# The lower halves of the last FFN's down weights: VectorE subtraction or accumulating DMA

## The chip, the cores and the metric

The kernel runs on one core of a Trainium2 chip. The metric is device time in microseconds (us) for one execution, the median of several runs. The core has four engines that matter here, each with its own instruction stream: TensorE (PE in the profile, with its weight loads as PEld), VectorE (DVE), ScalarE (ACT) and GpSimd (POOL). SyncE (SP) only issues DMAs. Engines wait for one another and for DMAs through semaphores. Sixteen DMA engines serve all queues of the core.

## The reference

The model is a two-layer decoder trunk on 256 tokens with a width of 2048. Layer 0 mixes by causal pooling, layer 1 by latent attention; each layer ends in a SwiGLU feed-forward network (FFN) with 5632 hidden columns. All tensors are float32. What matters for this change is the FFN:

```python
def swiglu(h, w_gate, w_up, w_down):
    return (jax.nn.silu(h @ w_gate) * (h @ w_up)) @ w_down
...
for i in range(DEPTH):
    ...
    h = modulate(rmsnorm(x, norm_ffn[i]), shift_f, scale_f)
    x = x + gate_f[:, None, :] * swiglu(h, ffn_gate[i], ffn_up[i], ffn_down[i])
return rmsnorm(x, final_norm)
```

## The kernel before

**Products in halves.** A weight matrix is read in units of 512 by 512, laid out as 128 partitions of 2048 float32 values, which is 1 MiB. TensorE multiplies in the type float32r, which keeps fewer bits than float32, so each operand is split: the upper half `hi` is the value rounded to float32r, and the lower half `lo` is the value less `hi`. A product is the sum of three: activation's upper half times `hi`, its lower half times `hi`, its upper half times `lo`. A unit therefore costs 3 parts x 4 slices of 128 x 2 token tiles = 24 matmuls of 128x512 at L420, and in each unit the eight that read `lo` come last. Only in the last unit of a sum they come earlier: there the two token tiles are done one after the other.

**How a unit gets ready.** `w_unit` (L382) takes one of the six `raw` buffers, has SP load the unit into it (L387) and calls `split` (L370). That takes two of the six `hl` buffers, lets ACT write `hi` as a copy of `raw` (L374), and lets DVE write `lo = raw - hi` (L376). Six `hl` buffers hold three units: the one in use and two ahead. A `raw` buffer comes free when both halves are made.

**The FFN of a layer.** There are 11 hidden chunks of 512 columns. The steps stand in a list by hand: `FFN_STEPS`, in which p is the gate and up projection of a chunk, t its transposition on TensorE, and d the down projection of a group of chunks. `GROUPS` has chunks 0 to 2, 3 to 5, 6 to 8, and 9 to 10:

```python
FFN_STEPS = "p0 p1 t0 p2 t1 p3 t2 p4 p5 d0 t3 t4 p6 t5 d1 p7 t6 p8 t7 p9 t8 d2 p10 t9 d3".split()
GROUPS = ([0, 1, 2], [3, 4, 5], [6, 7, 8], [9, 10])
```

A step `down(i)` loops over four output columns of 512 and, within each, over the chunks of the group, and adds the products of one column in two banks of PSUM (one for each token tile). Groups 0, 1 and 2 have 12 units each. After a column the banks go to the sums in `x`: by ACT in group 0 (L762), by DVE in the others (L764).

**Background work.** `split` begins with `tick()`, which at a planned rate issues other work: `Part.unit` loads 1 MiB of `mod_wt` into a `raw` buffer on the same SP queue (L210) and has DVE multiply and sum it (L211). In the last FFN this goes on until step p8. Two loads of the residual stream that was set aside (L613) fall into the time of d2 and p10.

**Order.** A scheduler places the instructions on each engine by priority; the halves have a raised one, and every engine runs its stream in order. POOL has little to do in the whole program: 30 busy instructions. Its only DMAs spread three gate rows (L297).

Of the kernel before, what the change touches and what calls it, by code (L numbers as in the profile page):

```python
# [9 lines left out]
F32 = mybir.dt.float32  # L10
# [3 lines left out]
AF = mybir.ActivationFunctionType  # L14
ALU = mybir.AluOpType
# [11 lines left out]
DEPTH = 2  # L27
# [31 lines left out]
GROUPS = ([0, 1, 2], [3, 4, 5], [6, 7, 8], [9, 10])  # L59
# [34 lines left out]
def tile_trunk(ctx: ExitStack, tc: tile.TileContext, a: dict, out: bass.AP):  # L94
    nc = tc.nc
    sync, act, dve, pe, pool = nc.sync, nc.scalar, nc.vector, nc.tensor, nc.gpsimd
# [7 lines left out]
    def nm(s):  # L104
        n_names[0] += 1
        return f"{s}_{n_names[0]}"

    def raw_t(shape, dt=F32):
        return work.tile(shape, dt, tag="raw", bufs=6, name=nm("raw"))

    def hl_t(shape, dt=F32R):
        return work.tile(shape, dt, tag="hl", bufs=6, name=nm("hl"))

    def act_t(shape, dt=F32R):
        return work.tile(shape, dt, tag="act", bufs=8, name=nm("act"))
# [10 lines left out]
    def ps_t():  # L126
        return psum.tile([P, CH], F32, tag="ps", name=nm("ps"))
# [195 lines left out]
    def pump(n):  # L323
        with tc.issue_after(behind[-1]) if behind else nullcontext():
            for _ in range(min(n, len(background))):
                background.pop(0).unit()
# [15 lines left out]
    def tick():  # L342
        credit[0] += rate[0]
        while credit[0] >= 1.0 and not held[0]:
            credit[0] -= 1.0
            if len(background) > goal[0]:
                pump(1)
# [8 lines left out]
    def flush(*ins):  # L356
        if not ins:
            while pending:
                pending.pop(0)[1]()
            return  # L360
        todo = [f for wait, f in pending if wait == 0]
        pending[:] = [(wait - 1, f) for wait, f in pending if wait]
        with ExitStack() as queue:
            for i in ins:
                queue.enter_context(tc.issue_after(i.ins))
            for f in todo:
                f()


    def split(r, shape):  # L370
        tick()
        hi, lo = hl_t(shape), hl_t(shape)
        with tc.high_priority(offset=100):
            hi_ins = act.activation(hi, r, AF.Copy)  # L374
        with tc.high_priority(offset=100):
            lo_ins = dve.tensor_tensor(out=lo, in0=r, in1=hi.bitcast(F32), op=ALU.subtract)  # L376
        flush(hi_ins, lo_ins)
        return hi, lo

    early, w_load = {}, [None]  # L380

    def w_unit(src):  # L382
        if repr(src) in early:
            return early.pop(repr(src))
        shape = [P, KL, CH]
        r = raw_t(shape)
        w_load[0] = sync.dma_start(r.rearrange("p k n -> p (k n)"), src)  # L387
        return split(r, shape)

    class Halved:  # L390
# [303 lines left out]
    def ffn_weights(l):  # L694
        return a["ffn_gate"][l], a["ffn_up"][l], a["ffn_down"][l]
# [40 lines left out]
    def ffn(l, hT, gate_name, begun, then):  # L736
        wd = ffn_weights(l)[2]
        mids, nat = {}, {}

        def project(c, which):  # L740
            if c in begun:
                begun[c][which].block(ND - 1, hT[ND - 1])
                return begun[c][which].result()
            return proj(ffn_weights(l)[which][:, c], hT)

        def transposed(c):
            m = act_t([P, 2, KL, T])
            for tok in range(NT):
                pt = ps_t()
                for f in range(KL):  # L750
                    pe.transpose(pt[:, f * P:(f + 1) * P], nat[c][tok][:, f * P:(f + 1) * P], ident)  # L751
                v = pt.rearrange("p (f t) -> p f t", f=KL)
                ts_ = slice(tok * P, (tok + 1) * P)
                act.activation(m[:, 0, :, ts_], v, AF.Copy)  # L754
                dve.tensor_tensor(out=m[:, 1, :, ts_], in0=v, in1=m[:, 0, :, ts_].bitcast(F32), op=ALU.subtract)  # L755
            mids[c] = m

        stream_end = []

        def gather(bank, sums, first):  # L760
            if first:
                act.activation(sums, bank, AF.Copy)  # L762
            else:
                dve.tensor_tensor(out=sums, in0=bank, in1=sums, op=ALU.add)  # L764

        def down(i):
            g = GROUPS[i]
            last = g[-1] == NF - 1
            if last:
                stat_start()  # L770
                end = stream_end[0]
                end.start(gates[gate_name])
            for j in range(ND):
                js = slice(j * CH, (j + 1) * CH)
                banks = [ps_t() for _ in range(NT)]
                if last and j == 0:
                    hold()
                if last and j == ND - 1:
                    weights = [w_unit(wd[c, j]) for c in g]
                    if l < DEPTH - 1:  # L780
                        then([(mids[c], hi, lo, c == g[0]) for c, (hi, lo) in zip(g, weights)], banks,
                             lambda tok: end.piece(banks[tok], tok, j))
                        continue
                    for tok in range(NT):
                        ends = tok == NT - 1
                        if not ends:
                            for c, (hi, lo) in zip(g, weights):
                                proj_unit(banks, mids[c], hi, lo, c == g[0], c == g[-1], (tok,))
                            end.piece(banks[tok], tok, j)
                            end.finish(tok)  # L790
                            end.rest_of(tok + 1)
                            continue

                        order = [(mids[c], w, i, k) for c, (hi, lo) in zip(g, weights)
                                 for w, i in ((hi, 0), (hi, 1), (lo, 0)) for k in range(KL)]
                        for bank, hs in ((banks[tok], slice(0, CH // 2)), (ps_t(), slice(CH // 2, CH))):
                            for n, (m, w, i, k) in enumerate(order):
                                pe.matmul(bank[:, :hs.stop - hs.start], lhsT=m[:, i, k, tok * P:(tok + 1) * P],
                                          rhs=w[:, k, hs], start=n == 0, stop=n == len(order) - 1)
                            end.section(bank, tok, hs)  # L800
                        end.finish_fast(tok)
                    continue
                for c in g:
                    hi, lo = w_unit(wd[c, j])
                    turning = last and j == 0 and c == g[0]
                    proj_unit(banks, mids[c], hi, lo, c == g[0], c == g[-1],
                              between=(lambda: transposed(g[-1])) if turning else None)
                for tok in range(NT):
                    if last:
                        pending.append((0, lambda bank=banks[tok], tok=tok, j=j: end.piece(bank, tok, j)))  # L810
                    else:
                        pending.append((0, lambda bank=banks[tok], sums=x[:, tok, js]: gather(bank, sums, i == 0)))

        def project_chunk(c):
            if c == ASIDE:
                stream_aside(l)
            if c == NF - 1:
                end = StreamEnd(l)
                stream_end.append(end)
                for n, wait in enumerate(KNOWN):  # L820
                    pending.append((wait, lambda n=n: end.known(n // NT, n % NT, gates[gate_name])))
            gb = project(c, GATE)
            nat[c] = []
            for tok in range(NT):
                sg = t2k([P, CH])
                pending.append((0, lambda sg=sg, bank=gb[tok]: act.activation(sg, bank, AF.Silu)))  # L826
                nat[c].append(sg)
            ub = project(c, UP)
            for tok in range(NT):
                dve.tensor_tensor(out=nat[c][tok], in0=ub[tok], in1=nat[c][tok], op=ALU.mult)  # L830

        for step in FFN_STEPS:
            {"p": project_chunk, "t": transposed, "d": down}[step[0]](int(step[1:]))
# [100 lines left out]
    scale = Strips(1, False, lambda v: with_bias(cols[:, C_AM0, :], v, 1, vcol[:, V_NM:V_NM + KD]))  # L934
# [451 lines left out]
    for j in range(ND):  # L1386
        if len(hmx) < ND:
            hidden_q()
        hi, lo = w_unit(a["w_dq"][j, 0])
# [132 lines left out]
    for g in range(3):  # L1522
        if g > 0:
            project_heads(g - 1)
        r, q_h, q_l = head_weights(g)
        uq[g] = q_h, q_l
        tick()
        with tc.high_priority(offset=100):
            hi_ins = act.activation(q_h, r, AF.Copy)
# [201 lines left out]
```

## Time and profile before

| What | Value |
|---|---|
| Median of 3 runs | 1903.12 us (1901.91 to 1905.33) |
| Profiled execution: span, first to last instruction | 1901.2 us |
| PE busy | 1850.5 us (97%) |
| DVE busy | 1418.4 us (75%) |
| ACT busy | 834.6 us (44%) |
| POOL busy | 21.7 us (1%) |
| DMA, over the span | 575.49 MB, mean 303 GB/s |

The profiled execution has no time of its own beside its span, the time from its first to its last instruction; that span lies 1.9 us under the median of the runs.

Reading it: each row of a group of instructions names the line, the engine and the operation, then the tiles written and read, the shape, the count, the busy time, the mean time of one in nanoseconds, and the idle time of the engine before them with what ended it. PE's busy time comes from modelled ends, since matmuls overlap; so a row can show 390 ns for a matmul while a new one starts sooner. A table by stretches of time gives, for each stretch, the busy us of each engine (with the number of instructions), the granted TensorE clock, the mean busy share of the 16 DMA engines, and the GB/s that they moved. "SPq" and "POOLq" are the queues on which DMAs are issued.

### The profile page before, as it was taken

What the parts mean: (1) busy time and instruction counts of PE and PEld (TensorE: products, weight loads), DVE (VectorE), ACT (ScalarE), POOL (GpSimd) and SP (SyncE); (2) the same over time, 40 slices, a digit from 0 to 9 for tenths busy, and PEclk for the clock granted to TensorE, in tenths of its full rate; (3) what the DMA queues carried; (4) which work ended last, traced back from release to release, by engine and by line L of the source; (5) the groups of instructions that cost most, each with busy time, mean ns of one, the idle gap of its engine ahead of it and who ended that gap; (6) DMA issues with size and microseconds to landing.
All of it is one profiled execution on the core that took longest, in us unless ns stands there. A gap on an engine that the chain in (4) does not pass through costs nothing.

```text
span 1901.2 us, 21797 instructions
## 1 busy us (share of the span) xinstructions
PE 1850.5 (97%) x8733; PEld 1501.9 (79%) x8733; DVE 1418.4 (75%) x1411; ACT 834.6 (44%) x914; POOL 21.7 (1%) x30
## 2 busy tenths in 40 slices
PE   7689999999999999999999999999999999999998
PEld 2256888888888888888889888888888888888886
DVE  1247799999889788897898886889785565644556
ACT  3125643453433343345776645634444433333343
POOL 0000000000000000000110000000000000000000
PEclk9989999999999999999999999999999999999999
DMA  9999998889999899994694585988776666655551
GB/s 399 417 419 410 381 368 332 317 308 375 411 351 394 341 381 360 392 418 178 221 368 164 185 324 223 385 321 335 260 268 243 245 242 243 246 219 201 220 199 44
DMA packets 80118, 575.49 MB, mean 303 GB/s; under 512 B 8929, under 2 KB 9361, under 8 KB 11281
## 3 DMA queue, kind: packets, MB, share of 16 engines
q1 hardware_dynamic: 79346, 570.68, 77.7%
q0 software_dynamic: 432, 3.15, 0.4%
q8 instruction: 68, 1.11, 0.2%
q10 hardware_dynamic: 240, 0.29, 0.0%
q14 instruction: 32, 0.26, 0.0%
HBM read 567.76 MB, written 6.32 MB: 302 GB/s over the span
## 4 chain that ended last, share of the span: by engine, by line
PE 94%; DMA 5%; ACT 0%; DVE 0%; SPq 0%; issue 0%; POOLq 0%; DVEq 0%; ACTq 0%
PE ps L420 80%; DMA raw<-in_mod_w_dram 4%; PE ps L429 2%; PE ps L1001 2%; PE ps L256 2%; PE ps L1354 1%; PE ps L751 1%; PE ps L1440 1%; PE ps L1546 1%; PE ps L1257 1%; DMA raw<-in_mod_block_dram 0%; PE ps L562 0%; PE ps L1443 0%; PE ps L196 0%; PE ps L1455 0%; PE ps L1495 0%
## 5 line engine op out<-in xcount | busy, mean ns | idle before, releaser
L420 PE MATMUL ps<-hl,act 128*128 128x512 f32 x6672 | 1522.6, 390 | 0.7 <-ACT act L754 0.7
L420 PEld LDWEIGHTS ps<-hl,act 128*128 128x128 f32 x6672 | 1250.8, 188 | 259.5 <-ACT act L754 0.9
L374 ACT ACTIVATE hl<-raw 128x2048 fp32r<-128x2048 f32 x285 | 545.5, 1918 | 644.7 <-PE ps L420 444.8
L376 DVE TENSOR_TENSOR hl<-raw,hl 128x2048 fp32r<-128x2048 f32 x285 | 652.2, 2290 | 234.0 <-ACT hl L374 232.2
L211 DVE SCALAR_TENSOR_TENSOR raw<-raw,s_row 128x2048 f32<-128x2048 f32 x168 | 383.4, 2285 | 1.3 <-DMA raw<-in_mod_wt_dram 1.2
L256 PE MATMUL ps<-raw,s_strip 128*32 128x512 f32 x392 | 59.0, 692 | 36.4 <-DMA raw<-in_mod_w_dram 35.4
L720 DVE TENSOR_TENSOR act<-ps,act 128x512 f32<-128x512 f32 x96 | 64.5, 685 | 17.9 <-PE ps L420 17.8
L256 PEld LDWEIGHTS ps<-raw,s_strip 128*32 128x32 f32 x392 | 9.1, 116 | 66.3 <-DMA raw<-in_mod_w_dram 43.3
L429 PE MATMUL ps<-hl,act 128*128 128x512 f32 x192 | 47.6, 400 | 0.6 <-DVE act L525 0.5
L429 PEld LDWEIGHTS ps<-hl,act 128*128 128x128 f32 x192 | 35.1, 188 | 10.3 <-ACT act L512 2.5
L754 ACT ACTIVATE act<-ps 128x512 fp32r<-128x512 f32 x44 | 23.7, 591 | 41.1 <-PE ps L751 29.0
L764 DVE TENSOR_TENSOR x<-ps,x 128x512 f32<-128x512 f32 x32 | 21.7, 690 | 23.1 <-PE ps L420 23.1
L542 DVE TENSOR_TENSOR hl<-raw,hl 128x2048 fp32r<-128x2048 f32 (+3 forms) x17 | 31.9, 1879 | 4.8 <-ACT hl L539 4.7
L830 DVE TENSOR_TENSOR t2k<-ps,t2k 128x512 f32<-128x512 f32 x24 | 16.5, 689 | 24.5 <-PE ps L420 24.5
L263 DVE COPY t2k<-ps 128x256 f32<-128x256 f32 x4 | 1.7, 425 | 44.0 <-ACT t2k L262 44.0
L826 ACT ACTIVATE t2k<-ps 128x512 f32<-128x512 f32 x24 | 14.2, 591 | 46.4 <-PE ps L420 46.4
L1001 PEld LDWEIGHTS ps<-act,act 128*128 128x128 f32 x128 | 24.4, 197 | 11.5 <-issue 8.4
L449 ACT ACTIVATE junk<-x 128x512 bf16<-128x512 f32 x23 | 14.4, 627 | 41.0 <-DVE x L634 23.9
L718 ACT ACTIVATE act<-ps 128x512 f32<-128x512 f32 x32 | 19.1, 596 | 29.2 <-PE ps L420 29.2
L1001 PE MATMUL ps<-act,act 128*128 128x256 f32 x128 | 31.5, 398 | 0.0
L755 DVE TENSOR_TENSOR act<-ps,act 128x512 fp32r<-128x512 f32 x44 | 28.4, 684 | 2.5 <-ACT act L754 2.5
L539 ACT ACTIVATE hl<-raw 128x2048 fp32r<-128x2048 f32 (+1 forms) x15 | 26.5, 1766 | 3.5 <-PE ps L420 3.5
(230 smaller groups left out, 984.7 us busy)
## 6 DMA issues: line engine op xcount, KB each, us to landing
raw<-in_mod_wt_dram SPq DMA_DIRECT2D x136, 1024.0 KB, 6.1
raw<-in_ffn_up_dram SPq DMA_DIRECT2D x88, 1024.0 KB, 5.5
raw<-in_ffn_down_dram SPq DMA_DIRECT2D x88, 1024.0 KB, 5.4
raw<-in_ffn_gate_dram SPq DMA_DIRECT2D x87, 1024.0 KB, 5.5
raw<-in_mod_w_dram SPq DMA_DIRECT2D x48, 1024.0 KB, 13.5
raw<-in_kv_mod_wt_dram SPq DMA_DIRECT2D x32, 1024.0 KB, 7.8
raw<-in_w_o_dram SPq DMA_DIRECT2D x16, 1024.0 KB, 5.4
raw<-in_mod_block_dram SPq DMA_DIRECT2D x8, 1024.0 KB, 12.5
```

Source lines behind the costliest of these rows:

```text
L211: dve.scalar_tensor_tensor(out=r, in0=r, scalar=1.0, in1=s_row, op0=ALU.mult, op1=ALU.mult, accum_out=self.sums[:, self.n:self.n + 1])
L256: pe.matmul(self.bank[m * STRIP:(m + 1) * STRIP, :], lhsT=weights(k), rhs=r[:, k, i, :], start=first, stop=last)
L374: hi_ins = act.activation(hi, r, AF.Copy)
L376: lo_ins = dve.tensor_tensor(out=lo, in0=r, in1=hi.bitcast(F32), op=ALU.subtract)
L420: pe.matmul(banks[tok], lhsT=t_[:, i, k, tok * P:(tok + 1) * P], rhs=w[:, k, :], start=first and n < len(part), stop=last and n >= len(ord ...
L429: pe.matmul(bank, lhsT=t_[:, i, k, tok * P:(tok + 1) * P], rhs=w[:, k, :], start=first and n == 0, stop=last and n == len(order) - 1)
L539: hid_ins[0] = act.activation(w[1], w[0], AF.Copy)
L542: dve.tensor_tensor(out=w[2][:, ks], in0=w[0][:, ks], in1=w[1][:, ks].bitcast(F32), op=ALU.subtract)
L720: dve.tensor_tensor(out=part, in0=banks[tok], in1=part, op=ALU.add)
L754: act.activation(m[:, 0, :, ts_], v, AF.Copy)
L755: dve.tensor_tensor(out=m[:, 1, :, ts_], in0=v, in1=m[:, 0, :, ts_].bitcast(F32), op=ALU.subtract)
L1001: pe.matmul(mixed[g][:, n % 2, :], lhsT=wp[g][:, k, ns], rhs=pool_all[g // 2][:, g % 2, k, :], start=k == 0, stop=k == KL - 1)
```

## The change

For the last layer's groups 0, 1 and 2, which is 36 units, a flag sends `w_unit` another way. SP loads the unit into `raw` as before and ACT writes `hi` as before. Then ACT writes `lo` too, as the negated `hi` (a copy from SBUF to SBUF with scale -1), and POOL issues a DMA that reads the same 1 MiB of weights from HBM again and adds it to `lo` in place. DVE's subtraction of these units is gone. Group 3, the projections and the first FFN keep the old way.

```diff
+    by_dma = [False]
...
         w_load[0] = sync.dma_start(r.rearrange("p k n -> p (k n)"), src)
+        if by_dma[0]:
+            tick()
+            hi, lo = hl_t(shape), hl_t(shape)
+            with tc.high_priority(offset=100):
+                hi_ins = act.activation(hi, r, AF.Copy)
+                act.activation(lo, hi.bitcast(F32), AF.Copy, scale=-1.0)
+                pool.dma_start(lo.rearrange("p k n -> p (k n)"), src, accum_op=ALU.add)
+            flush(hi_ins)
+            return hi, lo
         return split(r, shape)
...
         def down(i):
+            by_dma[0] = l == DEPTH - 1 and i < len(GROUPS) - 1
...
+            by_dma[0] = False
```

The streams of PE and SP keep their instructions and their order. On ACT, five units of d1 stand like this before:

```order
L374 ACTIVATE hl_11002<-raw_11000 128x2048
L374 ACTIVATE hl_11034<-raw_11032 128x2048
L374 ACTIVATE hl_11067<-raw_11062 128x2048
L374 ACTIVATE hl_11099<-raw_11097 128x2048
L374 ACTIVATE hl_11131<-raw_11129 128x2048
```

And the same five units of d1 on ACT now (L393 writes `hi`, L394 the negated copy):

```order
L393 ACTIVATE hl_11017<-raw_11015 128x2048
L394 ACTIVATE hl_11018<-hl_11017 128x2048
L393 ACTIVATE hl_11050<-raw_11048 128x2048
L394 ACTIVATE hl_11051<-hl_11050 128x2048
L393 ACTIVATE hl_11084<-raw_11079 128x2048
L394 ACTIVATE hl_11085<-hl_11084 128x2048
L393 ACTIVATE hl_11117<-raw_11115 128x2048
L394 ACTIVATE hl_11118<-hl_11117 128x2048
L393 ACTIVATE hl_11150<-raw_11148 128x2048
L394 ACTIVATE hl_11151<-hl_11150 128x2048
```

Each unit has two ACT instructions in place of one, the second right behind the first. On DVE, at the same place of d1, the subtractions stand among evictions (L764) and background work (L211) before:

```order
L376 TENSOR_TENSOR hl_11035<-raw_11032,hl_11034 128x2048
L764 TENSOR_TENSOR x<-ps_10903,x 128x512
L764 TENSOR_TENSOR x<-ps_10904,x 128x512
L376 TENSOR_TENSOR hl_11068<-raw_11062,hl_11067 128x2048
L211 SCALAR_TENSOR_TENSOR raw_11193,sums_9830<-raw_11193,s_row 128x2048
L376 TENSOR_TENSOR hl_11100<-raw_11097,hl_11099 128x2048
L376 TENSOR_TENSOR hl_11132<-raw_11129,hl_11131 128x2048
```

On DVE in d1 now, only the evictions and the background work are left:

```order
L774 TENSOR_TENSOR x<-ps_10915,x 128x512
L211 SCALAR_TENSOR_TENSOR raw_11214,sums_9830<-raw_11214,s_row 128x2048
L774 TENSOR_TENSOR x<-ps_10916,x 128x512
L774 TENSOR_TENSOR x<-ps_11013,x 128x512
L211 SCALAR_TENSOR_TENSOR raw_11314,sums_9830<-raw_11314,s_row 128x2048
L774 TENSOR_TENSOR x<-ps_11014,x 128x512
```

On POOL, from the end of d1 to the start of d2, the DMAs that add now stand in the order of the units, with the spreading of the last gate row between the two groups:

```order
L395 DMA hl_11218<-in_ffn_down_dram 128x2048
L395 DMA hl_11251<-in_ffn_down_dram 128x2048
L395 DMA hl_11282<-in_ffn_down_dram 128x2048
L297 DMA gate_11871<-row_958 128x2048
L395 DMA hl_12135<-in_ffn_down_dram 128x2048
L395 DMA hl_12166<-in_ffn_down_dram 128x2048
L395 DMA hl_12197<-in_ffn_down_dram 128x2048
```

Before, the gate row's DMA was POOL's only work there; now each unit has a DMA of 1 MiB on POOL's queue that waits for ACT.

## Prediction

> **What bounds the kernel now.** I read the page first (busy times, then the chain that ended last), then the table by stretches over the three groups of the change, the groups of instructions and the waits of the same time, and last the timeline around the start of d2. The page says that TensorE is the bound of the whole:
>
> ```profile
> span 1901.2 us, 21797 instructions
> ...
> PE 1850.5 (97%) x8733; PEld 1501.9 (79%) x8733; DVE 1418.4 (75%) x1411; ACT 834.6 (44%) x914; POOL 21.7 (1%) x30
> ...
> PE 94%; DMA 5%; ACT 0%; DVE 0%; SPq 0%; issue 0%; POOLq 0%; DVEq 0%; ACTq 0%
> ```
>
> DVE, which the change relieves, is on none of the chain. Such shares are means over stages, so the stages themselves have to be read. The next table has, in this order, a stretch of the first FFN in which the DMA engines are full, group d0 of the last FFN, the projections between d0 and d1, groups d1 and d2, and the end of the program:
>
> ```profile
> core 0: us, PE busy (x) PEld busy (x) DVE busy (x) ACT busy (x) POOL busy (x), PEclk, DMA share, GB/s
> 800.00:850.00 50.00, 50.00 (x227) 41.48 (x226) 44.07 (x40) 21.26 (x14) 0.00 (x0) 1.00 1.01 420
> 1424.00:1490.00 66.00, 66.00 (x293) 54.66 (x292) 38.87 (x24) 26.71 (x20) 0.00 (x0) 1.00 0.66 239
> 1494.00:1538.00 44.00, 44.00 (x199) 36.45 (x198) 25.51 (x18) 17.57 (x15) 0.00 (x0) 1.00 0.63 228
> 1538.00:1604.00 66.00, 66.00 (x296) 54.74 (x294) 40.80 (x29) 23.82 (x15) 0.00 (x0) 1.00 0.68 254
> 1737.00:1803.00 66.00, 66.00 (x294) 54.68 (x293) 35.18 (x25) 23.80 (x15) 0.00 (x0) 1.00 0.61 222
> 1800.00:1850.00 50.00, 49.30 (x224) 40.70 (x223) 29.63 (x24) 19.30 (x13) 0.00 (x0) 1.00 0.59 211
> 1850.00:1901.20 51.20, 42.77 (x215) 36.23 (x213) 35.90 (x52) 18.69 (x28) 1.11 (x2) 0.95 0.11 41
> ```
>
> In each group PE is busy for 66.00 of 66.00 us at a granted clock of 1.00. DVE is busy for 35 to 41 us and waits for the rest, ACT for 24 to 27. The DMA engines are at 0.61 to 0.68 and move 222 to 254 GB/s, where 420 GB/s is what they move when full. So TensorE has no gap here that anything could close, and the resource with the least room behind it is the DMA engines.
>
> The groups of instructions from d0 to d2 show the same from the engines' side:
>
> ```profile
> L420 PE MATMUL ps<-hl,act 128*128 128x512 f32 x1650 | 375.5, 389 | 0.0
> ...
> L376 DVE TENSOR_TENSOR hl<-raw,hl 128x2048 fp32r<-128x2048 f32 x69 | 158.2, 2292 | 141.7 <-ACT hl L374 141.6
> L374 ACT ACTIVATE hl<-raw 128x2048 fp32r<-128x2048 f32 x69 | 132.3, 1918 | 211.6 <-PE ps L420 211.6
> ```
>
> The matmuls of L420 had an idle time of 0.0 before them over 1650. ACT's copies wait for PE (211.6 us), that is for a free `hl` buffer, and DVE's subtractions wait for ACT. Everybody waits for TensorE, nobody for DVE.
>
> **The change, part by part.** *What it removes.* 36 subtractions on DVE, at 2292 ns each: 82.5 us of DVE time. By the rows above this lies wholly beside PE, which waits for none of it. Its worth is 0.
>
> *ACT's second copy.* A copy of the same shape takes 1918 ns, so ACT gets 36 x 1.918 = 69.0 us more, 23.0 in each group. From 26.71 us of 66 it goes to 49.7: it fits. The copy needs the `lo` buffer of three units before, so ACT waits there, and the next unit's upper half and the evictions of d0 are queued behind it. They have the lead that the timeline shows, so I cost this at nothing; without the lead each would add up to 1.9 us to its unit.
>
> *The latency of one unit.* These are rows of the timeline where d2 starts, with the start and the length in us first:
>
> ```profile
> 1695.29 27.65 SPq L387 DMA_DIRECT2D raw<-in_ffn_down_dram  x6
> ...
> 1723.78 1.92 ACT L374 ACTIVATE hl<-raw 128x2048 fp32r<-128x2048 f32 x1 [3.52 <-PE ps L420]
> ...
> 1729.22 1.92 ACT L374 ACTIVATE hl<-raw 128x2048 fp32r<-128x2048 f32 x1 [3.52 <-PE ps L420]
> ...
> 1737.07 5.25 PE L420 MATMUL ps<-hl,act 128*128 128x512 f32 x22
> ...
> 1740.99 1.92 ACT L374 ACTIVATE hl<-raw 128x2048 fp32r<-128x2048 f32 x1 [2.54 <-PE ps L420]
> ```
>
> PE starts on d2 at 1737.07. The copies of units 1 and 2, each released by PE, are 5.44 us apart: that is PE's time for a unit, 0.227 us for each of its 24 matmuls. The copy at 1740.99 is that of unit 4, since three units fit in the buffers. PE comes to unit 4 at 1737.07 + 3 x 5.44 = 1753.4 and to its `lo` after 16 matmuls, at 1757.0. Under the change: `hi` until 1742.9, negated copy until 1744.8, then POOL's DMA. The one DMA that POOL issues before, with its time from issue to landing:
>
> ```profile
> L297 POOL DMA_DIRECT2D gate<-row x3: 572/614/698, 465.2 to 1696.0; - x3
> ...
> DMA to landing us min/median/max: 5.7/6.8/9.5
> ```
>
> At 6.8 us the sum lands at 1751.6, at 9.5 at 1754.3: 5.4 or 2.7 us ahead of its use. In the last unit of a column the `lo` is read after 8 matmuls, 1.8 us earlier, and still in time. So the longer chain alone costs nothing; its cover is 2.7 us at worst.
>
> *POOL's queue.* The gate row's DMA now stands behind the adds of d1, and the adds of d2 behind it. It was issued at 1696.0, and the first add of d2 would be at 1723.78 + 2 x 1.92 = 1727.6, so 31 us cover it: nothing. If that cover went, d2's first units would be late by the difference.
>
> *The DMA engines' work.* This is the term that decides. When full they move 420 GB/s, so 1 MiB takes 1.0486 / 0.420 = 2.50 us. The present load of the groups is, in MiB, 239 x 66 / 1048.6 = 15.0, then 16.0 and 14.0 (12 weight units, and background or stream loads), which is 37.6, 40.0 and 34.9 us of full DMA time. The change adds 12 accumulating DMAs to each group. No row shows one, so I bound it by passes of 1 MiB. Low end: one pass, 2.50 us, as if the add were free and the old value of `lo` cost nothing to fetch. High end: three passes, 7.50 us, if fetching the weight, fetching the old value and writing the sum do not overlap. In between: two passes, 5.00 us, since an engine must read two inputs for each output, while plain loads already write as they read. I take two, the count of the bytes to be read; a gain below one pass is excluded, since the weights are still read.
>
> What can be put off is the lead of the loads. Six unit loads start at 1695.29, and the first unit's copy starts at 1723.78, so loads are 28.5 us, or five units, ahead. A group can let five loads slip, 5 x 2.50 = 12.5 us, before PE is short. Between d0 and d1 the DMA engines are free for 0.37 x 44 = 16 us, enough to win that back, and from d1 to d2 for longer.
>
> | Passes | DMA work of d0, d1, d2 (us) | Over 66 us each | Less 12.5 each |
> |---|---|---|---|
> | 1 | 67.6, 70.0, 64.9 | 1.6, 4.0, none | 0 |
> | 2 | 97.6, 100.0, 94.9 | 31.6, 34.0, 28.9 | 57.0 |
> | 3 | 127.6, 130.0, 124.9 | 61.6, 64.0, 58.9 | 147.0 |
>
> The Trainium skill bears on this in "Collectives: The Full Stack", under Part 3, "Why 7× under link rate — side-by-side accounting": a reducing DMA emits two read descriptors for each chunk on the same ring, and by its measurement runs 1.93 times slower than a copy. By that figure the 12 DMAs would be an estimated 57.9 us in each group and the whole 50.7 us slower; by the only row here, that of plain loads, the sum would be 0. No run here shows which.
>
> **Sum.** 82.5 us off DVE: 0. 69.0 us onto ACT: 0. Latency: 0. DMA work: +57.0. The profiled execution would go from 1901.2 to 1958.2, and the median, 1.9 above its span, from 1903.1 to 1960.1. The price is paid in PE's waits for `lo` in d0 to d2, about 19 us in each.
>
> **Rivals.** *The add is nearly free (one pass), and nothing changes.* For it: the load then fits by 1.6 to 4.0 us of overrun against a lead of 12.5, and the latency by 2.7. Against it: the old value of `lo` has to come from somewhere. It decides up to the point where work less lead equals 66, which for d1 is 12 x A = 66 + 12.5 - 40.0, or A = 3.2 us, 1.28 passes. Time 1903, so not slower; chance 0.26.
>
> *Three passes or nearly.* For it: a read, a read and a write that depend on one another. Against: the plain loads show reads and writes overlapped. It gives 1903.1 + 147.0 = 2050.1; chance 0.16, with 0.03 beyond it.
>
> *The work fits, but landing is late.* If POOL's issue or the landing of an adding DMA takes some 4 us more than the 9.5 us above, the cover of 2.7 is gone in each of 36 units while the buffers let only three be under way: 1.3 us for every third unit at the least, 12 x 1.3 = 16, so about 1919. For: the three gate rows spread from 5.7 to 9.5. Against: the median leaves 5.4. Chance 0.06.
>
> *Relief on DVE brings something.* The place would be the end, where PE idles 0.7 us from 1800 and 8.4 from 1850; evictions and subtractions there are not touched, though, and DVE enters it no earlier than PE does. All of it would make 1894. Chance 0.04.
>
> *That it does not do what it says* is excluded: the streams hold 36 DMAs more on POOL and 36 subtractions fewer on DVE.
>
> **How the numbers follow.** Two passes (about 1.5 to 2.5) get 0.45, for the two inputs; one pass 0.26, three 0.16, beyond 0.03, late landing 0.06, faster 0.04. Some 0.2% is what a measurement of this kernel can tell from no change, 3.8 us. Faster is then 0.04; same is the one-pass case, 0.26; slower is 0.45 + 0.16 + 0.03 + 0.06 = 0.70. The range goes from the undisturbed time, 1902, to three passes, 2050; it leaves out the faster case, what lies beyond three passes and about half of that case, 0.15.
>
> **What would show it.** Right: in d0 to d2 the idle time before L420 is about 19 us a group and is ended by the DMA into `hl`; the DMA share there is near 1.0; POOL's adding DMAs land in over 9.5 us; DVE loses some 27 us in each group; d3 is as before. Wrong: PE at 66 of 66 in the groups with a DMA share under 0.95 would mean that the add is cheap; a DMA share below 0.9 with PE waiting would mean latency, not work; a stall of some 50 us a group, three passes or more.

## The result and the profile after

| | Before | After |
|---|---|---|
| Time, median (us) | 1902.51 (1901.07 to 1905.33) | 1977.92 (1976.30 to 1978.11) |
| Ratio, 95% interval | | 1.0394 (1.0379 to 1.0409) |
| Span of the profiled execution (us) | 1901.2 | 1975.4 |

The change makes the kernel slower by 75.4 us, where the forecast was 57.0; the time lies inside the forecast range of 1902 to 2050. These are the lines of the page after that answer to those of before:

```profile
span 1975.4 us, 21934 instructions
...
PE 1880.1 (95%) x8733; PEld 1518.6 (77%) x8733; DVE 1335.8 (68%) x1375; ACT 902.8 (46%) x950; POOL 53.5 (3%) x66
...
q0 software_dynamic: 5616, 40.90, 9.7%
...
PE 82%; DMA 12%; issue 4%; ACT 1%; DVE 1%; SPq 0%; POOL 0%; POOLq 0%; DVEq 0%; ACTq 0%
...
L430 PE MATMUL ps<-hl,act 128*128 128x512 f32 x6672 | 1550.2, 394 | 48.1 <-DMA hl<-in_ffn_down_dram 47.4
...
L393 ACT ACTIVATE hl<-raw 128x2048 fp32r<-128x2048 f32 x36 | 69.0, 1917 | 96.1 <-PE ps L430 96.1
...
hl<-in_ffn_down_dram POOLq DMA_DIRECT2D x36, 1024.0 KB, 15.1
```

DVE is busy for 82.6 us less and ACT for 68.2 more, as costed, and neither is what moved the time. The share of the DMA engines in the chain went from 5 to 12%. The matmuls (now L430) waited for nothing in the groups before and wait 47.4 us for the adding DMAs now. The span grew by 74.2 us: PE's idle time went from 50.7 to 95.3 (+44.6), and its busy time from 1850.5 to 1880.1 (+29.6) with the same 8733 matmuls. The second part is a lower granted clock, which the next table of stretches shows. Its rows go from the issue of the first adding DMA of d0, d1 and d2 to the landing of the last:

```profile
core 0: us, PE busy (x) PEld busy (x) DVE busy (x) ACT busy (x) POOL busy (x), PEclk, DMA share, GB/s
1419.20:1511.80 92.60, 75.34 (x304) 59.45 (x303) 13.87 (x15) 50.42 (x34) 10.66 (x12) 0.94 1.03 282
1554.30:1648.10 93.80, 78.12 (x318) 62.17 (x316) 15.90 (x17) 46.87 (x26) 10.57 (x12) 0.93 1.03 286
1777.80:1871.10 93.30, 79.27 (x318) 63.12 (x316) 12.10 (x13) 46.86 (x26) 10.56 (x12) 0.91 1.03 285
...
1877.00:1975.40 98.40, 89.24 (x424) 74.57 (x422) 63.90 (x72) 36.93 (x41) 1.11 (x2) 0.97 0.32 118
```

The DMA engines stood at 0.61 to 0.68 in the groups before and stand at 1.03 now, with fewer bytes per second than the 420 GB/s of a stretch full of plain loads. PE is idle for 14 to 17 us of each stretch, and the granted clock is 0.91 to 0.94. The last row is all that follows d2, that is p10, t9, d3 and the end of the program: 98.40 us with 424 matmuls, as in the profile of before, in which it lasts from 1802.80 to the end at 1901.20. So all of the loss lies ahead of p10.

Where it lies is read by counting matmuls: the time at which PE has started equally many in both profiles. First the profile of before, from the start to four such points (the start of d0, a point between d0 and d1, one between d1 and d2, the end of d2):

```profile
0.00:1420.90 1420.90, 1379.35 (x6601) 1110.50 (x6602) 1140.62 (x1201) 648.21 (x773) 20.02 (x27) 0.99 0.86 334
0.00:1534.70 1534.70, 1493.15 (x7112) 1204.94 (x7113) 1206.69 (x1243) 697.28 (x810) 20.02 (x27) 0.99 0.84 327
0.00:1640.20 1640.20, 1598.65 (x7581) 1292.41 (x7582) 1270.66 (x1285) 735.77 (x833) 20.02 (x27) 0.99 0.83 321
0.00:1802.80 1802.80, 1761.25 (x8311) 1427.28 (x8312) 1354.44 (x1340) 797.63 (x874) 20.60 (x28) 0.99 0.81 313
```

Then the same counts of matmuls (one more in the second row, 0.2 us) in the profile after:

```profile
0.00:1420.00 1420.00, 1381.20 (x6601) 1112.81 (x6602) 1138.65 (x1201) 650.66 (x775) 20.81 (x28) 0.99 0.86 335
0.00:1560.00 1560.00, 1503.84 (x7113) 1211.53 (x7114) 1176.84 (x1231) 723.57 (x824) 31.82 (x41) 0.99 0.86 330
0.00:1690.00 1690.00, 1618.05 (x7581) 1303.42 (x7582) 1215.40 (x1261) 781.10 (x857) 41.29 (x51) 0.98 0.87 327
0.00:1877.00 1877.00, 1790.85 (x8311) 1444.00 (x8312) 1271.94 (x1304) 865.86 (x910) 52.41 (x64) 0.98 0.87 321
```

The profile after is 0.9 us ahead at the start of d0, then 25.1, 49.8 and 74.2 behind. Each group loses nearly the same: 26.0, 24.7 and 24.4 us, 75.1 in all.

The timeline of PE in d2 shows how (start, length, and in brackets the idle time before and what ended it; the view ends at 1840, in the middle of the last burst):

```profile
1786.84 9.32 PE L430 MATMUL ps<-hl,act 128*128 128x512 f32 x40
1796.47 3.91 PE L430 MATMUL ps<-hl,act 128*128 128x512 f32 x16 [0.30 <-DMA hl<-in_ffn_down_dram]
1803.83 19.47 PE L430 MATMUL ps<-hl,act 128*128 128x512 f32 x72 [3.46 <-DMA hl<-in_ffn_down_dram]
1826.74 13.64 PE L430 MATMUL ps<-hl,act 128*128 128x512 f32 x52 [3.43 <-DMA hl<-in_ffn_down_dram]
```

PE runs for three units (72 matmuls, as many units as the `hl` buffers hold) and stops. From 1803.83 to 1826.74 these and the wait behind them take 22.9 us, where three units took 3 x 5.44 = 16.3.

### The profile page after: what moved, and what is told of

It reads as the page before. It is cut to its first block, busy times and chain, and to the rows that moved or that the text cites. A ratio compares the mean times of both kernels' runs of the same rounds, so it can differ in the third digit from the quotient of the medians.

```text
span 1975.4 us, 21934 instructions
## 1 busy us (share of the span) xinstructions
PE 1880.1 (95%) x8733; PEld 1518.6 (77%) x8733; DVE 1335.8 (68%) x1375; ACT 902.8 (46%) x950; POOL 53.5 (3%) x66
## 4 chain that ended last, share of the span: by engine, by line
PE 82%; DMA 12%; issue 4%; ACT 1%; DVE 1%; SPq 0%; POOL 0%; POOLq 0%; DVEq 0%; ACTq 0%
PE ps L430 68%; DMA hl<-in_ffn_down_dram 8%; DMA raw<-in_mod_w_dram 3%; PE ps L439 2%; PE ps L1013 2%; PE ps L256 1%; PE ps L1366 1%; PE ps L761 1%; PE ps L1452 1%; PE ps L1558 1%; PE ps L1269 1%; DMA raw<-in_mod_block_dram 0%; PE ps L572 0%; PE ps L1455 0%; PE ps L196 0%
## 5 line engine op out<-in xcount | busy, mean ns | idle before, releaser
L430 PE MATMUL ps<-hl,act 128*128 128x512 f32 x6672 | 1550.2, 394 | 48.1 <-DMA hl<-in_ffn_down_dram 47.4
L430 PEld LDWEIGHTS ps<-hl,act 128*128 128x128 f32 x6672 | 1264.9, 190 | 320.3 <-issue 55.5
L376 DVE TENSOR_TENSOR hl<-raw,hl 128x2048 fp32r<-128x2048 f32 x249 | 569.1, 2287 | 159.0 <-ACT hl L374 157.4
L211 DVE SCALAR_TENSOR_TENSOR raw<-raw,s_row 128x2048 f32<-128x2048 f32 x168 | 383.1, 2283 | 136.0 <-DMA raw<-in_mod_wt_dram 101.2
L393 ACT ACTIVATE hl<-raw 128x2048 fp32r<-128x2048 f32 x36 | 69.0, 1917 | 96.1 <-PE ps L430 96.1
L394 ACT ACTIVATE hl<-hl 128x2048 fp32r<-128x2048 f32 x36 | 68.9, 1915 | 6.6 <-PE ps L430 5.8
L439 PE MATMUL ps<-hl,act 128*128 128x512 f32 x192 | 47.7, 401 | 0.6 <-DVE act L535 0.5
L395 POOL DMA_DIRECT2D hl<-in_ffn_down_dram x36 | 31.8, 883 | 554.6 <-ACT hl L394 275.3
L439 PEld LDWEIGHTS ps<-hl,act 128*128 128x128 f32 x192 | 35.1, 188 | 10.3 <-ACT act L522 2.5
L764 ACT ACTIVATE act<-ps 128x512 fp32r<-128x512 f32 x44 | 23.9, 591 | 38.5 <-PE ps L761 29.0
L838 ACT ACTIVATE t2k<-ps 128x512 f32<-128x512 f32 x24 | 14.2, 591 | 48.7 <-PE ps L430 48.7
## 6 DMA issues: line engine op xcount, KB each, us to landing
raw<-in_mod_w_dram SPq DMA_DIRECT2D x48, 1024.0 KB, 12.9
hl<-in_ffn_down_dram POOLq DMA_DIRECT2D x36, 1024.0 KB, 15.1
```

The costliest lines, as they stand in the source:

```text
L211: dve.scalar_tensor_tensor(out=r, in0=r, scalar=1.0, in1=s_row, op0=ALU.mult, op1=ALU.mult, accum_out=self.sums[:, self.n:self.n + 1])
L394: act.activation(lo, hi.bitcast(F32), AF.Copy, scale=-1.0)
L395: pool.dma_start(lo.rearrange("p k n -> p (k n)"), src, accum_op=ALU.add)
L430: pe.matmul(banks[tok], lhsT=t_[:, i, k, tok * P:(tok + 1) * P], rhs=w[:, k, :], start=first and n < len(part), stop=last and n >= len(ord ...
L439: pe.matmul(bank, lhsT=t_[:, i, k, tok * P:(tok + 1) * P], rhs=w[:, k, :], start=first and n == 0, stop=last and n == len(order) - 1)
```

## The experiments

The question was which property of the adding DMA costs the time: the work that it makes for the DMA engines (W in the expectations), or its latency and the chain through ACT and POOL (L). Later runs ask why the loss is 75 and not 57.

**The same DMA without the add:**

```diff
-                pool.dma_start(lo.rearrange("p k n -> p (k n)"), src, accum_op=ALU.add)
+                pool.dma_start(lo.rearrange("p k n -> p (k n)"), src)
```

> The changed kernel with POOL's 36 DMAs as plain copies of the weights into lo (no add); everything else stays, so lo is wrong. Theory W (work: the DMA engines are full because an add costs two passes, 0.628 us for each packet of 8192 bytes against 0.309): the DMAs cost one pass, 12 x 2.5 + 30 + 7.5 = 67.5 us of DMA work for a group of 66 us, which the lead covers: 1902 to 1908 us, packets at 0.309 us. Theory L (latency: one unit's chain of ACT copy, POOL issue, software queue and landing is too long for three units of buffers): the chain is the same but for the add, so at least half of the loss stays, 1940 us or more. If the packets stay at 0.628, the price is that of the cast to float32r or of the software queue and not of the add.

Measured: 1905.18 against 1902.22, ratio 1.0019 (1.0009 to 1.0029). The lines of its page on the DMA queue and on the matmuls:

```profile
q0 software_dynamic: 5616, 40.90, 5.6%
...
L430 PE MATMUL ps<-hl,act 128*128 128x512 f32 x6672 | 1524.1, 390 | 1.5 <-ACT act L764 0.7
```

The negated copies, POOL's queue, the waits and the 36 MiB are all still there, and PE waits 0.6 us for them in all. What costs is the add in the DMA. The queue's shares give its price. Before, 3 DMAs took 0.4% of 1901.2 us, 7.6 us. After, it is 9.7% of 1975.4, 191.6, so an add takes (191.6 - 7.6) / 36 = 5.11 us of all 16 engines; here a copy takes (5.6% of 1903.7 - 7.6) / 36 = 2.75. The price of an add is not the same to the hundredth everywhere: by the same reckoning it is 5.41 in the run without the units' loads below (10.6% of 1907.4).

**No DMA at all.** `lo` stays the negated upper half; the line of `pool.dma_start` is left out.

> The changed kernel without POOL's 36 DMAs: lo stays the negated hi, so the output is wrong; ACT's second copy and the missing DVE subtractions stay. Theory W and theory L: nothing is left that PE waits for, 1901 to 1905 us. Rival A (ACT's second copy and what is queued behind it is the loss): 1978 us stays.

Measured: 1901.80 against 1902.22, ratio 0.9999 (0.9990 to 1.0009). DVE's 36 subtractions are gone, ACT's 36 copies are there, and nothing is gained or lost. This run prices both terms at once, at zero.

**Half of each sum by DMA, half on DVE.**

```diff
-                act.activation(lo, hi.bitcast(F32), AF.Copy, scale=-1.0)
-                pool.dma_start(lo.rearrange("p k n -> p (k n)"), src, accum_op=ALU.add)
+                act.activation(lo[:, :KL // 2], hi[:, :KL // 2].bitcast(F32), AF.Copy, scale=-1.0)
+                half = KL // 2
+                pool.dma_start(lo[:, :half].rearrange("p k n -> p (k n)"), src[:, :half * CH], accum_op=ALU.add)
+                dve.tensor_tensor(out=lo[:, half:], in0=r[:, half:], in1=hi[:, half:].bitcast(F32), op=ALU.subtract)
```

> Half of each lo (two of four slices) by negated copy and adding DMA, the other half by DVE's subtraction; the result is complete. Theory W: adds are 12 x 2.5 = 30 us for a group, the DMA work 67.5 to 70 us against 66, covered by the lead: 1902 to 1908 us. Theory L: the fixed parts of the chain stay and only the transfer is halved: 1920 us or more.

Measured: 1905.29 against 1902.22, ratio 1.0015 (1.0005 to 1.0024). 36 adds of 512 KB landed in a median of 10.1 us, and PE waited 2.3 us for them in all:

```profile
L432 PE MATMUL ps<-hl,act 128*128 128x512 f32 x6672 | 1523.6, 390 | 3.1 <-DMA hl<-in_ffn_down_dram 2.3
```

Half of the work costs almost nothing, so the price isn't in proportion to the adds. The DMA engines are at 1.00 to 1.01 here too, from the first add of a group to the landing of its last; full engines alone cost almost nothing as long as their work still fits in the time of a group and its lead.

**The adds without the loads.** The 36 units' own loads are left out, and `hi` is made from a tile that is there anyway. The add still brings `lo` to the weights less whatever `hi` is, so the sum of the halves remains the weights.

```diff
-        r = raw_t(shape)
-        w_load[0] = sync.dma_start(r.rearrange("p k n -> p (k n)"), src)
+        if by_dma[0]:
+            r = s_row.rearrange("p (k n) -> p k n", k=KL)
+        else:
+            r = raw_t(shape)
+            w_load[0] = sync.dma_start(r.rearrange("p k n -> p (k n)"), src)
```

> The changed kernel without the raw loads of the 36 units (hi is made from another tile that lies in SBUF, so the output is wrong); the 36 adding DMAs stay as they are. Theory W: 12 x 5.02 = 60.2 us of adds and about 7.5 of other loads a group, 67.7 against 66: 1902 to 1908 us, with adds that land in 8 to 9 us. Theory L, and a rival by which the adding DMAs are themselves too slow or run one after the other: 1978 us stays, or most of it, since nothing in the chain of lo is changed.

Measured: 1908.90 against 1902.22, ratio 1.0034 (1.0023 to 1.0045). Every add of the changed kernel is there with its chain, and they land sooner, since no load of their unit shares the engines with them:

```profile
L433 PE MATMUL ps<-hl,act 128*128 128x512 f32 x6672 | 1524.2, 390 | 4.4 <-DMA hl<-in_ffn_down_dram 3.7
...
hl<-in_ffn_down_dram POOLq DMA_DIRECT2D x36, 1024.0 KB, 8.7
```

PE's wait falls from 47.4 to 3.7 us. The stretch of the adds of d2, in the columns above:

```profile
1733.80:1804.30 70.50, 70.50 (x317) 58.47 (x316) 10.38 (x12) 46.87 (x26) 10.53 (x12) 1.00 0.98 196
```

The adds with the other loads of the time just fit, at 0.98 and PE busy throughout (in d0 and d1 PE is idle for 3.2 and 0.4 us). With the plain copies and the half adds this settles the cause: the adds and the units' loads together are more than the engines do in the time of a group. The chain alone, at these landings, costs at most the 6.7 us that are left.

**PE kept busy in its waits.** Is the lower clock a loss of its own? Eight matmuls are put ahead of each of the 36 units (the first products are taken twice), 36 x 8 x 0.227 = 65.3 us of work more:

```diff
+            if by_dma[0]:
+                order = order[:4 * len(part)] + order
```

> The changed kernel with eight more matmuls in front of each of the 36 units (the first products are done twice, so the output is wrong): 36 x 8 x 0.227 = 65.3 us more work for TensorE, in the place where it waits. With no DMA in the way this would be 1902 + 65 = 1967 us. Theory W (the DMA engines' work alone sets the time of a group, 7.5 us for a unit): the filling costs nothing and saves nothing, 1976 to 1980 us. Theory C (the clock, granted at 0.5 for 3.4 us behind each long wait, is part of the loss): filled waits keep the clock up and the time falls by part of some 20 us, to about 1968. If waits and work simply add up: 1978 + 65 = 2043 us.

Measured: 1980.42 against 1901.64, ratio 1.0415 (1.0400 to 1.0431). Its stretches of the adds:

```profile
1419.90:1511.00 91.10, 89.11 (x391) 72.94 (x390) 12.29 (x14) 50.38 (x34) 10.63 (x12) 1.00 1.01 273
1553.80:1641.70 87.90, 87.61 (x392) 72.35 (x391) 13.27 (x16) 44.95 (x25) 10.55 (x12) 1.00 1.02 273
1782.50:1876.00 93.50, 92.35 (x410) 75.64 (x408) 11.85 (x13) 46.86 (x26) 10.53 (x12) 1.00 1.03 285
```

PE is busy for nearly all of the stretches, at a clock of 1.00, and the ratio is that of the changed kernel but for 0.2%, with intervals that overlap. The 29.6 us of slower matmuls are no second loss: PE would have waited for the DMA in them anyway.

**Only d2 changed.**

```diff
-            by_dma[0] = l == DEPTH - 1 and i < len(GROUPS) - 1
+            by_dma[0] = l == DEPTH - 1 and i == len(GROUPS) - 2
```

> The change in group d2 alone; the result is complete. Theory W with the cover as the trace of the changed kernel shows it (some 8 us, from the first add's issue to PE's first need): 1902 + 20 to 21 = 1923 us. With the cover that the prediction took (12.5 us of loads that slip): 60.3 + 35 - 66 - 12.5 = 17, so 1919 us. If the three groups act on one another (a debt carried along), d2 alone would cost less than the 20.7 us that it costs in the changed kernel.

Measured: 1926.38 against 1901.64, ratio 1.0129 (1.0114 to 1.0144), 24.7 us for one group. The expectation had 20 to 21, from an earlier estimate of 20.7 for d2 in the changed kernel; the count of matmuls gives 24.4 there, and the two agree. So what d2 pays is its own overrun, with no debt carried over from d0 and d1; those two were not run alone.

**The loads put behind the adds.** On POOL's queue a unit's load cannot overtake an add:

```diff
-        w_load[0] = sync.dma_start(r.rearrange("p k n -> p (k n)"), src)
+        w_load[0] = (pool if by_dma[0] else sync).dma_start(r.rearrange("p k n -> p (k n)"), src)
```

> The changed kernel with the raw loads of the 36 units issued on POOL's queue, in one line with the adds, in place of SP's queue; the result is complete. Question: why the loads' lead of five units covered less than 12.5 us a group. Theory T (two queues take turns, so loads that nobody waits for yet hold up adds that PE waits for): in one line an add waits only for what stands ahead of it, and the time falls to 1960 to 1972 us. Theory W alone (the sum of the work, in whatever order): 1976 to 1980 us. Slower than 1980 would mean that POOL's own waits in order cost more than the turns did.

Measured: 1987.15 against 1901.64, ratio 1.0453 (1.0436 to 1.0471), slower than the changed kernel. Its waits show a new one, of POOL for a free `raw` buffer, with the adds queued behind it. The longest of the 13, 109.9 us, lies between d1 and d2, where POOL has no add to issue; the others come to 78.1:

```profile
POOL raw L388 <- DVE hl L376: 188.0, 13, 109.9
```

So this run doesn't tell what a yielding load would be worth.

**Two units of three by DMA.** `by_dma` is false for the last unit of each three in d0 to d2.

```diff
+                    by_dma[0] = l == DEPTH - 1 and not last and c != g[-1]
```

> The change for two of three units: the last chunk of each column keeps DVE's subtraction; the result is complete. Theory W: 8 x 5.02 = 40.2 us of adds a group, so 77.8, 80.2 and 75.1 us of DMA work against 66, less a cover of 7 to 8 each: about 4, 7 and 2 us, so 1913 to 1917 us. Theory L (each adding DMA costs PE the same wait): two thirds of 75, 1952 us.

Measured: 1933.10 against 1901.64, ratio 1.0165 (1.0150 to 1.0180), a miss on the slow side. A part of it stands in the timeline at the end of d1:

```profile
1600.77 2.29 DVE L211 SCALAR_TENSOR_TENSOR raw<-raw,s_row 128x2048 f32<-128x2048 f32 x1 [16.43 <-DMA raw<-in_mod_wt_dram]
...
1602.99 2.29 DVE L376 TENSOR_TENSOR hl<-raw,hl 128x2048 fp32r<-128x2048 f32 x1
...
1605.33 12.98 PE L430 MATMUL ps<-hl,act 128*128 128x512 f32 x45 [8.47 <-DVE hl L376]
```

Background work on DVE waits 16.43 us for a load that the adds have made late, a subtraction that PE needs stands behind it, and PE waits 8.47 us. On a mix of both ways, PE is exposed to DVE's queue too. In all, the matmuls of L430 wait 10.6 us for DVE, 8.6 for the adds and 1.9 for ACT. The expectation of 11 to 15 us was for the adds alone, so the waits for DVE and ACT, 12.5 us, are most of the 16 to 20 that it missed; the rest is not settled.

**Loads made to yield.** One buffer of `raw` (in a second kernel two) is taken up ahead of each of the last six units of a group, so that the loads run fewer units ahead:

```diff
+        if narrow[0]:
+            for _ in range(1):
+                dve.tensor_copy(raw_t(shape)[:, 0, 0:1], s_col[:, 0:1])
...
+                    narrow[0] = by_dma[0] and j * len(g) + c - g[0] >= 6
```

> The changed kernel in which the loads must slip: from the seventh unit of each group on, a unit takes two of the six raw buffers (one is only touched by a one-column copy on DVE), so the loads' lead falls from five units to two or three towards the group's end and comes back behind it; the result is complete. Question: was the prediction's cover of 12.5 us a group (five loads put off) right in kind, and unused only because loads go out as soon as a buffer is free? Theory S (yes): two to three loads of 2.5 us less fall into each group, so 5 to 7.5 us less a group, 1956 to 1963 us. If a load put off saves nothing (the adds are slow by themselves, or their turn does not come sooner): 1976 to 1980 us. If units then come late: over 1980.

> As the run with the short lead, with two touched buffers for each unit from the seventh of a group on, so only two buffers of six carry units and the lead falls to one or two. Theory S: three to four loads less in each group, 7.5 to 10 us, 1948 to 1956 us, unless a raw unit comes too late for its copy, which would show as ACT's L393 waiting for a DMA. If a load put off saves nothing: 1976 to 1980 us.

Measured: 1973.79 against 1902.14, ratio 1.0376 (1.0361 to 1.0392), and with two 1973.58, 1.0380 (1.0363 to 1.0397). Both miss. The stretches of the adds of the first show that the edit hardly did what it was for:

```profile
1420.60:1510.70 90.10, 73.68 (x304) 58.35 (x302) 9.86 (x16) 50.37 (x34) 10.64 (x12) 0.96 1.03 279
1554.50:1644.70 90.20, 75.62 (x318) 60.38 (x316) 16.30 (x23) 46.84 (x26) 10.55 (x12) 0.96 1.03 281
1773.40:1866.80 93.40, 76.27 (x318) 60.29 (x316) 12.88 (x18) 46.85 (x26) 10.54 (x12) 0.96 1.03 286
```

279 GB/s x 90.10 us / 1.0486 MB is 24.0 MiB, then 24.2 and 25.5. In the changed kernel the three are 24.9, 25.6 and 25.4. Only 2.2 MiB were put off, worth 2.2 x 2.50 = 5.5 us; the ratios differ by 3.4 us, and their intervals overlap. The kernel with two buffers did hardly more: 279, 279 and 284 GB/s in 90.2, 90.4 and 93.1 us are 24.0, 24.1 and 25.2 MiB.

**A sum of half the width.** The DMA adds into a bfloat16 view of `raw`, 4096 bytes per partition where the source has 8192; `lo` stays the negated upper half, so the lower half of the product is left out.

```diff
-                pool.dma_start(lo.rearrange("p k n -> p (k n)"), src, accum_op=ALU.add)
+                pool.dma_start(r.rearrange("p k n -> p (k n)").bitcast(BF16)[:, :D], src, accum_op=ALU.add)
```

> Why an add costs two passes. As the changed kernel, but POOL's 36 DMAs add the float32 weights to a bfloat16 view of the raw tile, which nothing reads any more; lo stays the negated hi, so the output is wrong, and PE waits for no add. The source has 8192 bytes a row as before, the old value and the sum 4096. Theory R (the old value is read through the same engine, by its bytes): 0.31 + 0.16 = 0.46 to 0.47 us for a row, so queue q0 takes about 7.5% of the 16 engines' span. Theory E (the adder goes by elements, 2048 a row as before): 0.63 us, about 10%. If it is 5 to 6%, the old value costs nothing in this form. The time itself stays near 1902 to 1910 us, since only buffers of raw are held longer.

Measured: 1924.80 against 1902.34, ratio 1.0118 (1.0089 to 1.0147). The queue of the adds, what the matmuls waited for, and a wait of DVE from 1400 to 1850 us:

```profile
q0 software_dynamic: 5616, 22.02, 7.8%
...
L430 PE MATMUL ps<-hl,act 128*128 128x512 f32 x6672 | 1528.6, 391 | 16.8 <-DVE hl L376 16.1
```

```profile
DVE raw L211 <- DMA raw<-in_mod_wt_dram: 122.4, 9, 30.2
```

(7.8% of 1924.0 - 7.6) / 36 = 3.96 us for an add. Bytes read by the engines are 1 MiB for the copy, 1.5 here (weights and half as much of old sum) and 2 for the add; the prices are 2.75, 3.96 and 5.11. They follow the bytes read; what is written (1, 0.5, 1 MiB) doesn't order them. The run changes the type as well as the width, so a price of the cast is not told apart; the half adds, which keep the types of the changed kernel, come to (5.5% of 1904.5 - 7.6) / 36 = 2.70 us for 1 MiB read. The time misses its 1902 to 1910 and tells nothing of this. PE waits 16.1 us for DVE's subtractions. The likely reason, not tested, is that the `raw` buffers are held until the DMA lands, so that the background loads come late, and DVE waits 122.4 us for them with subtractions queued behind.

## Why the prediction was right, and where its sum was short

The forecast was right in kind: the DMA engines' work decides, and an add is two passes of it. The range alone says little for it, as it runs from no change to three passes.

*The 82.5 us off DVE and the 69.0 us onto ACT.* Both worth 0, as forecast: without the DMA the ratio is 0.9999.

*The longer chain and POOL's queue.* Worth little: with plain copies the time moves by 0.19%, without the loads by 0.34%. The late-landing rival foresaw 16 us from it. The median landing is 15.1 us in the changed kernel and 8.7 with the adds alone, so it is late because the units' loads share the engines. (In the last unit of a column, whose `lo` is read 1.8 us earlier, the cover of the chain by the prediction's own figures was 0.9 us and not "2.7 us at worst"; nothing here turned on it.)

*An add is two passes, 5.00 us.* It measured 5.11. The one-pass rival is what the plain copy shows (2.75 us, and 0.6 us of wait of PE for it); three passes are out. The Trainium skill's rule in "Collectives: The Full Stack", Part 3, told there of ReduceScatter against AllGather, that a reducing DMA emits two read descriptors and so runs 1.93 times slower than a copy, agrees with this trace: 5.11 / 2.75 = 1.86. Its estimate of 50.7 us for the whole was lower than the 75.4 measured for the same reason as the forecast's.

*The cover of 12.5 us in each group.* This is the term that was mis-sized. The prediction let "five loads slip" in each group before PE is short. With 5.11 for an add, the work of a group exceeds 66 us by 32.9, 35.3 and 30.2; the groups lost 26.0, 24.7 and 24.4. So the cover was 6.9, 10.6 and 5.8 us, 23.3 in all, where 37.5 were taken off. Of the 18.1 us that the forecast lacks, 37.5 - 23.3 = 14.2 are this, and 36 x 0.11 = 4.0 the price of an add. The 23.3 is a remainder, and it hangs on the 5.11: at the 5.41 of the run without loads more of the lack would fall to the price and less to the cover. What shows that the term was wrong is the loads themselves.

The timeline of d2 shows that their lead was not spent. First SP's queue, then the copy of the last unit on ACT:

```profile
1787.28 24.32 SPq L388 DMA_DIRECT2D raw<-in_ffn_down_dram  x4
1816.22 21.93 SPq L388 DMA_DIRECT2D raw<-in_ffn_gate_dram  x4
1843.27 13.50 SPq L388 DMA_DIRECT2D raw<-in_ffn_up_dram  x2
```

```profile
1854.49 1.92 ACT L393 ACTIVATE hl<-raw 128x2048 fp32r<-128x2048 f32 x1 [8.83 <-PE ps L430]
```

The last load of d2 was issued by 1811.6, and its copy began at 1854.49, 43 us later. At 22.9 us for three units that is 5.6 units, where the lead was five before. Not one unit was given up. SP issues a load as soon as a `raw` buffer comes free, one for each unit that ACT and PE use up; after the last of d2 it went on with loads of the next projection (gate and up, p10), in the time in which d2's adds were wanted. The loads kept pace, 24.9, 25.6 and 25.4 MiB less 12 of adds, so 12.9, 13.6 and 13.4 in each stretch, where the forecast had 10, 11 and 9 in each group (of 85 us and about that; the stretches are some 8 longer). Against the 15.0, 16.0 and 14.0 of before, 2.1, 2.4 and 0.6 loads were put off, not five.

What cover there was, d2 shows too: its first add was issued at 1777.8 and PE came to it at 1786.84, a start of 9.0 us; the rest after the last landing, until 1877.0, took 5.9. So d2 took 93.3 - 9.0 + 5.9 = 90.2 us on PE, against 1802.8 - 1737.07 = 65.7: 24.5 more. That loads which yield would bring back the 14.2 was not shown; of the three kernels meant to do it, two put off some 2 to 3 MiB, and one ran into another wait.

*The signs named beforehand.* PE's waits for the DMA into `hl` were forecast as about 19 us a group; PE is idle for 17.3, 15.7 and 14.0 us in the stretches, 47.0 in all, where the page has 47.4 us of waits for the adds. That they come near 19 is in part luck: a group lost some 25 us, and the lower clock, which the forecast did not have, took the rest of it as slower matmuls. The DMA share is 1.03; the adds land in a median of 15.1 us, over 9.5. DVE's busy time in d0 to d2 falls by 25.0, 24.9 and 23.1 us (from the stretches of 66 us to the longer ones now), about the 27. What follows d2 lasts as long as before.

## What to carry to other kernels

Moving arithmetic from an engine that nobody waits for to the DMA engines gained nothing here and used up the room that the DMA engines had. Count a DMA that adds as the bytes that it reads, old sum and new addend, and hold that against the stage in which it runs. A prefetch queue that refills as buffers come free did not yield to the other transfers here; count its lead as cover only where something stops its issues. The half-size run shows the scale: 0.5 MiB per unit by DMA fitted into the room of the groups, 1 MiB did not.

## What the runs showed of the hardware that was not expected

- The price of an adding DMA by the bytes read: 2.75, 3.96 and 5.11 us of all engines for 1, 1.5 and 2 MiB, and 2.70 for the half adds, which read 1 MiB and write half of it. The packets in the traces say the same by their medians: 0.325 us for a copy of 8192 bytes on POOL's queue, 0.327 for a half add (4096 new, 4096 old), 0.478 for the narrow sum (8192 and 4096), 0.628 for an add (8192 and 8192).
- A wait of 3.46 us costs PE more than the wait. The 72 matmuls behind it took 19.47 us where 72 x 0.227 = 16.3 is usual, and the 52 behind the wait of 3.43 took 13.64 in place of 11.8: surpluses of 3.1 and 1.8 us, as if the first 6.3 and 3.7 us ran at half the clock. The granted clock shows it: 0.50 from 1803.83 to 1809.90 and 1.00 from there to 1823.30. By the Trainium skill, "TensorE: Matmul & The Clock Gate", Part 1, the clock falls to half after an idle window of about 3.4 us and comes back after a busy one of that length, on windows that run freely; these rows agree with about two such windows behind the first wait and about one behind the second. Behind a wait of 1.65 us, which ended at 1437.17, the granted clock stayed at 1.00. Here it cost nothing in the end, as the run with filled waits shows, because the DMA was the bound.
- The same add landed in a median of 8.7 us without its unit's loads and in 15.1 with them, though the engines were at 0.98 to 0.99 in the one case and 1.03 in the other.
